# Wider matmuls for q, k and v: two narrow ones become one of 512 columns

## The chip, the cores and the metric

One core of a Trainium2 chip runs the whole program. The metric is device time in microseconds, from runs of the compiled kernel. TensorE (PE in the profile) multiplies 128x128 weights, loaded by a load instruction of their own (PEld), with a moving operand of up to 512 columns; it accumulates in PSUM, of which the kernel has eight buffers of 128x512 fp32. VectorE (DVE), ScalarE (ACT) and GpSimd (POOL) do the element-wise work, and the SP queue issues nearly all transfers from HBM.

## What is computed

Two decoder layers on 512 tokens of width 1024. Each has a token mixer and a squared-ReLU MLP, modulated by shift, scale and gate vectors that come from a conditioning vector (the adaLN products, "ada"). The parts that matter here, cut from the reference:

```python
# layer 0: the even mixer
proj = u @ w_in          # xr 512, yr 512, q 256, k 256, v 512, g 512, zl 16 columns
h = rg_lru(causal_dwconv(xr, ...), ...)
o = gla_chunked(q, k, v, log_alpha)          # 4 heads, chunks of 64 tokens
mix = concat([h * gelu(yr), rms_norm(o) * silu(g)]);  y = mix @ w_out
# layer 1: forgetting attention, 16 heads of 64
proj = u @ w_in          # q, k, v, g of 1024 columns each, 16 forget logits
q = rms_norm(q per head) * 64 ** -0.5;  k = rms_norm(k per head)
s = q @ k.T + f_cum[t] - f_cum[s], causal;  o = softmax(s) @ v
y = (o * sigmoid(g)) @ w_out
```

## The kernel before

**Products in three parts.** For fp32 precision each operand is split into a rounded high half and a low half, and a product is three matmuls: high by high, high by low, low by high (`mm3`). u is kept split and transposed (`uh`, `ul`; 8 blocks of 128 rows of the contraction). Projections whose result stands with tokens on partitions (`proj_tok`) take 128 tokens of u as weights and stream the columns of the weight matrix: 8 blocks x 3 = 24 matmuls for a token tile.

**Weights.** `plan_weights` lists all pieces of the weight matrices in the order of use, 1 MB each in the stages of this change. `w_dma` loads a piece into one of two staging buffers (`ws`); `w_pre` splits the next piece: ScalarE rounds it into `wh` (cast), VectorE subtracts for `wl`, in two tiles each, with four buffers for each of `wh` and `wl`, so two pieces exist at a time; `w_take` hands the next piece to its user and calls `w_pre` itself when the piece isn't split yet. A "tok" piece is 256 columns over the whole contraction of 1024 rows.

**Even mixer.** A string (`order`, L1051) writes out the order of the steps by hand: `q0` is a q product, `p` is `w_pre`, `t` a step of the ada products, `e` transposes of k, `R` the LRU gates, `s` scores, `g` the gate products, `S` the states, and so on. `v0` to `v7` are the products of v: four token tiles for the first 256 columns, then four for the second. Each is copied to its half of the tile `VV`.

**Attention.** The heads are worked through in groups j of four (256 columns of q, k and v). `stream` yields the projection units in order: q's four token tiles, k's, v's, for j = 1 to 3, then the gates. Group 0 is done before the heads begin. Strings (`orders`, L1532) mix one unit (`u`) at a time with the attention steps of a head: scores (`a`), decay (`d`), normalisation (`n`), transposes of the probabilities (`t`), values (`v`) and the stacking of the next q and k (`0` to `3`). `qk_units` puts two token tiles of q (or k) side by side into one PSUM buffer of 512 columns, and copies, squares and sums them; after all four tiles an rsqrt on VectorE and two multiplications on GpSimd normalise them.

Within these orders the tile framework still schedules: an engine's instruction order is fixed when the kernel is built, by priority of program order among what its own timing model holds ready. Helpers record all operations, so the profile gives one line (L50) for all; names of tiles tell them apart: `pqk` is q and k of the attention layer, `pfv` its v, `pfg` its gates, `pv` the even mixer's v, `pg` its gates, `pw` the output projections.

Of the kernel before, what the change touches and what calls it, by code (L numbers as in the profile page):

```python
# [8 lines left out]
F32 = mybir.dt.float32  # L9
F32R = mybir.dt.float32r  # L10
BF16 = mybir.dt.bfloat16
I32 = mybir.dt.int32
AF = mybir.ActivationFunctionType
ALU = mybir.AluOpType
AX = mybir.AxisListType
# [3 lines left out]
P = 128  # L19
D = 1024  # L20
S = 512
NT = S // P
# [4 lines left out]
RMS_EPS = 1e-6  # L27
# [7 lines left out]
WS_BUFS = 2  # L35
# [38 lines left out]
class Trunk:  # L74
# [19 lines left out]
    def s2(self, name, dtype=F32):  # L94
        return self.sp.tile([P, S], dtype, tag="s2", name=name)
# [220 lines left out]
    def plan_weights(self):  # L316
        i = self.i
        L = []
        win = i["ev_w_in"][0]
        L += [("ch", win, 1024, 256), ("ch", win, 1280, 256), ("tok", win, 1536), ("tok", win, 1792),  # L320
              ("ch", win, 2048, 256), ("ch", win, 2304, 256), ("ch", win, 640, 128), ("ch", win, 768, 256)]

        def out(w, n):
            for h in range(2):
                for b in range(2):
                    L.append(("half", w, h, b, n))

        def mlp(l):
            w1, w2 = i["mlp_w1"][l], i["mlp_w2"][l]
            up = lambda b: [("ch", w1, b * 512, 256), ("ch", w1, b * 512 + 256, 256)]  # L330
            dn = lambda b: [("rows", w2, b * 512, 2 * l + 1), ("rows", w2, b * 512 + 256, 2 * l + 1)]
            L.extend(up(0))
            for b in range(1, 8):
                L.extend(up(b) + dn(b - 1))
            L.extend(dn(7))

        self.wsmall = set()

        def alternate(n0):
            for q in range(n0, len(L)):  # L340
                if (q - n0) // 2 % 2:
                    self.wsmall.add(q)

        n0 = len(L)
        out(i["ev_w_out"][0], 0)
        mlp(0)
        alternate(n0)
        win = i["od_w_in"][0]
        tok = lambda m, j: ("tok", win, m * D + j * 256)
        L += [tok(0, 0), tok(1, 0), tok(2, 0)]  # L350
        for j in range(1, 4):
            L += [tok(0, j), tok(1, j), tok(2, j)]
        L += [("ch", win, 3 * D + j * 256, 256) for j in range(4)]
        n0 = len(L)
        out(i["od_w_out"][0], 2)
        mlp(1)
        alternate(n0)
        self.wlist, self.n_dma, self.n_split, self.n_take = L, 0, 0, 0
        self.wstage, self.wready = {}, {}

    def w_dma(self):
        d = self.wlist[self.n_dma]
        kind, w = d[0], d[1]
        if kind == "ch":
            shape, src = (KC, d[3]), w[:, d[2]:d[2] + d[3]]
        elif kind == "tok":
            shape, src = (KC, 256), w[:, d[2]:d[2] + 256]
        elif kind == "half":
            shape, src = (4, 512), w[d[3] * 512:d[3] * 512 + 512, d[2] * 512:d[2] * 512 + 512]
        else:  # L370
            shape, src = (2, D), w[d[2]:d[2] + 256, :]
        st = self.wp.tile([P, *shape], F32, tag="ws", bufs=WS_BUFS, name="ws")
        self.nc.sync.dma_start(st, src.rearrange("(k p) f -> p k f", p=P))
        self.wstage[self.n_dma] = st
        self.n_dma += 1
# [23 lines left out]
    def w_pre(self, eng=None):  # L399

        nc = self.nc
        if self.n_split >= len(self.wlist):
            return
        while self.n_dma < min(self.n_split + WS_BUFS, len(self.wlist)):
            self.w_dma()
        d = self.wlist[self.n_split]
        st = self.wstage.pop(self.n_split)
        kind = d[0]
        small = self.n_split in self.wsmall
        if kind == "ch":  # L410
            r = [self.split(st[:, :, m * P:m * P + P], P, small, eng) for m in range(d[3] // P)]
        elif kind == "tok":
            r = [x for h in range(2) for x in self.split(st[:, 4 * h:4 * h + 4, :], 256, small, eng)]
        elif kind == "half":
            r = []
            for a in range(2):
                r += self.split(st[:, 2 * a:2 * a + 2, :], 512, small, eng)
        else:
            r = []
            for k in range(2):  # L420
                for h in range(2):
                    s = st[:, k, h * 512:h * 512 + 512]

                    if d[2] >= DFF - 512:
                        nc.gpsimd.tensor_tensor(s, s, self.gates[d[3]][h], op=ALU.mult)
                r.append(self.split(st[:, k:k + 1], 512, small, eng))
        self.wready[self.n_split] = r
        self.n_split += 1
# [327 lines left out]
    def even(self):  # L756
        nc, tc, i, s2 = self.nc, self.tc, self.i, self.s2
# [14 lines left out]
        for m, nm in enumerate(("ev_rg_wa", "ev_rg_wx")):  # L772
            src = i[nm][0].rearrange("(q two) a b -> two a q b", two=2)
# [100 lines left out]
        W = {}  # L874
# [20 lines left out]
            nc.vector.tensor_tensor(ke[m], pk[m], E3[m], op=ALU.mult)  # L895

        V = [VV[:, t] for t in range(NT)]
        KE, kts = {}, {}

        def ke_t(t):  # L900

# [25 lines left out]
                AT[t, par] = at  # L927

        def v_proj(q):
            w2, t = q // 4, q % 4  # L930
            if t == 0:
                W["v"] = self.w_take()
            pt = self.ps("pv")
            self.proj_tok(pt[:, 0:256], W["v"], t)
            nc.scalar.copy(V[t][:, w2 * 256:w2 * 256 + 256], pt[:, 0:256])

        sg = {}

# [90 lines left out]
        ssq = [self.tiny.tile([P, 8], F32, tag="ss8", name="ss") for _ in range(2)]  # L1029
# [9 lines left out]
        def gla_put(h):  # L1039
            pt = self.ps("pot")  # L1040
            for t in range(NT):
# [6 lines left out]
        steps = dict(q=q_proj, D=decays, c=conv, M=lambda: nc.vector.tensor_copy(cm, cf), p=self.w_pre, t=self.tick,  # L1048
                     Q=q_decay, k=k_proj, K=k_decay, G=lambda: gelu(0, acc_ps[4]), v=v_proj, R=rg_gates, e=ke_t, s=scores,
                     g=silu, S=states, B=rg_sqrt, o=outs, n=norms, C=rg_scan, r=rg_put, y=yr, h=gla_put)  # L1050
        order = ("q0 c0 D M q1 p c1 t Q k0 p c2 K0 t k1 c3 K1 t G v0 p t e0 v1 R0 t e2 e1 v2 t v3 t e3 v4 "  # L1051
                 "p t s0 v5 t s1 R1 v6 t s2 v7 g0 t s3 t R2 p g1 R3 S0 t S2 g2 B p o0 o1 n0 t g3 C p t r0 "
                 "o2 o3 n2 y1 t y2 p t h0 p h2 h3 y3 t h1")
        for x in order.split():
            steps[x[0]](*[int(y) for y in x[1:]])
# [187 lines left out]
    def fox(self, rest):  # L1243
        nc, tc, i, s2 = self.nc, self.tc, self.i, self.s2
        win = i["od_w_in"][0]
# [18 lines left out]

            return unit

        def qk_units(j, m):

            w = self.w_take()
            pts = {}  # L1270
            QK[j, m] = [s2("qt") for _ in range(2)]
            ssq = self.tiny.tile([P, 16], F32, tag="ssq", name="ssq")

            def unit(t):
                b = t // 2
                if t % 2 == 0:
                    pts[b] = self.ps("pqk")
                pt, qt = pts[b], QK[j, m][b]
                self.proj_tok(pt[:, (t % 2) * 256:(t % 2) * 256 + 256], w, t)
                if t == 0:  # L1280
                    self.w_pre()
                if t % 2 == 0:
                    return
                sq = s2("sq")
                nc.scalar.copy(qt, pt)
                nc.scalar.activation(sq, pt, AF.Square)
                nc.vector.tensor_reduce(ssq[:, 8 * b:8 * b + 8], heads(sq), op=ALU.add, axis=AX.X)
                if b == 0:
                    return
                nc.vector.tensor_scalar(ssq, ssq, 1.0 / 64.0, RMS_EPS, op0=ALU.mult, op1=ALU.add)  # L1290
                r = self.rsqrt(ssq, 16)
                for q in range(2):
                    x = heads(QK[j, m][q])
                    rb = r[:, 8 * q:8 * q + 8].rearrange("p (a o) -> p a o", o=1).broadcast_to([P, 8, 64])
                    nc.gpsimd.tensor_tensor(x, x, rb, op=ALU.mult)

            return unit

        def stack(j, pr, m):

            pt = self.ps("pqt")
            for t in range(NT):
                c0 = (t % 2) * 256 + pr * P
                nc.tensor.transpose(pt[:, t * P:t * P + P], QK[j, m][t // 2][:, c0:c0 + P], self.ident)
            h0 = 4 * j + 2 * pr
            for hd in range(2):
                a, b = hd * 64, 64 - hd * 64
# [152 lines left out]


        wfs = forget_weights()
        u0 = qk_units(0, 0)
        u1 = qk_units(0, 1)
        for t in range(NT):
            u0(t)
            u1(t)
            if t == 0:
                rest(2)
            if t == 1:  # L1470
                rest(3)
        cols = forget()
        OG += [self.u8(f"og{k}", F32) for k in range(2)]
# [7 lines left out]

        def stream():
            for j in range(1, 4):
                for make in (lambda: qk_units(j, 0), lambda: qk_units(j, 1), lambda: v_units(j)):
                    u = make()
                    for t in range(NT):
                        yield lambda: u(t)
            for j in range(4):
                u = g_units(j)
                for m in range(2):  # L1490
                    for half in range(2):
                        yield lambda: u(m, half)
# [36 lines left out]
            "2": lambda h: stack(h // 4 + 1, 1, 0) if h < 12 else None,  # L1529
            "3": lambda h: stack(h // 4, 1, 1),  # L1530
        }
        orders = ("aduntu3uv", "datunuuv", "adnu0ut1uv", "audntu2uv")  # L1532
        for h in range(16):
            j, e = h // 4, h % 4
            for c in orders[e]:
# [61 lines left out]
```

## Time and profile before

| | us |
|---|---|
| median of 3 runs | 1263.17 (1262.27 to 1264.21) |
| profiled execution, its time | 1266.51 |
| its span, first to last instruction | 1264.8 |
| TensorE busy | 1224.6 |
| VectorE busy | 908.8 |
| ScalarE busy | 590.2 |
| GpSimd busy | 512.9 |

The profile is of one execution. Busy times count what an engine executes; matmuls overlap each other, so the distance between the starts of two tells what one costs in a row of them. A wait is put down to what ended it. The granted clock is that of TensorE, 1.00 being 2.4 GHz.

### The profile page before, as it was taken

To read this page: it belongs to the slowest core of one execution; us is meant where nothing else is said; L and a number is where in the kernel's file an instruction comes from. 1 tells how busy PE (TensorE), PEld (TensorE's weight loads), DVE (VectorE), ACT (ScalarE), POOL (GpSimd) and SP (SyncE) were. 2 spreads that over 40 slices of the span, in tenths; PEclk is the share of its full clock that TensorE was granted. 3 is DMA by queue.
4 is the path that set the end of the run, shared out by engine and by line. 5 is a ranking of instruction groups with operands and counts; after the bars stand their busy time and mean duration, and the time that the engine had idled before them with its cause. 6 is when DMAs were issued, how large, how long until landed. Compare 5 with 4: busy or idle time off the path is not lost. (4 is left out here: it accounts for less than half of the span.)

```text
span 1264.8 us, 17847 instructions
## 1 busy us (share of the span) xinstructions
PE 1224.6 (97%) x6543; PEld 1044.2 (83%) x6543; DVE 908.8 (72%) x1423; ACT 590.2 (47%) x1044; POOL 512.9 (41%) x524
## 2 busy tenths in 40 slices
PE   6999899999999999999999999999899999999997
PEld 5787678888888888888999999887888788888886
DVE  7689898768877866879578878778768744543656
ACT  3476653452453544432567767753453342322321
POOL 3665523346330321474266558558437000000166
PEclk9999999999999999999999999999999999999999
DMA  9657416163666466524232332343262624232311
GB/s 316 186 199 267 173 61 198 56 230 119 240 224 233 145 195 227 182 67 124 81 101 85 92 93 52 113 153 106 79 233 72 211 67 133 81 117 70 133 34 67
DMA packets 126409, 177.52 MB, mean 140 GB/s; under 512 B 9270, under 2 KB 82644, under 8 KB 126322
## 3 DMA queue, kind: packets, MB, share of 16 engines
q1 hardware_dynamic: 126210, 176.33, 42.4%
q8 instruction: 52, 0.85, 0.3%
q14 instruction: 35, 0.29, 0.1%
q10 hardware_dynamic: 112, 0.05, 0.0%
HBM read 172.10 MB, written 4.26 MB: 139 GB/s over the span
## 5 line engine op out<-in xcount | busy, mean ns | idle before, releaser
L50 DVE TENSOR_TENSOR wl<-ws,wh 128x512 fp32r<-128x512 f32 (+1 forms) x255 | 269.3, 1081 | 67.7 <-ACT wh L50 63.4
L50 ACT CAST wh<-ws 128x1024 fp32r<-128x1024 f32 (+2 forms) x271 | 207.5, 808 | 200.5 <-PE p L50 81.4
L50 PE MATMUL p<-uh,wh 128*128 128x512 f32 (+1 forms) x576 | 206.2, 366 | 0.0
L50 PE MATMUL p<-uh,wl 128*128 128x512 f32 (+1 forms) x576 | 205.9, 365 | 0.0
L50 PE MATMUL p<-wh,hh 128*128 128x512 f32 (+1 forms) x516 | 201.0, 390 | 0.0
L50 PE MATMUL p<-wh,hl 128*128 128x512 f32 (+1 forms) x516 | 200.0, 388 | 0.0
L50 PE MATMUL p<-wl,hh 128*128 128x512 f32 (+1 forms) x516 | 199.9, 387 | 0.0
L50 PE MATMUL p<-ul,wh 128*128 128x512 f32 (+1 forms) x576 | 192.9, 366 | 0.0
L50 POOL TENSOR_TENSOR acc<-acc,ast 128x512 f32<-128x512 f32 x70 | 102.9, 1470 | 203.3 <-ACT ast L50 108.4
L50 DVE TENSOR_TENSOR h<-r 128x512 f32<-128x512 f32 x64 | 53.6, 840 | 123.6 <-ACT r L50 123.6
L50 PEld LDWEIGHTS p<-uh,wl 128*128 128x128 f32 x576 | 108.6, 189 | 17.5
L50 PEld LDWEIGHTS p<-uh,wh 128*128 128x128 f32 x576 | 108.6, 189 | 17.6
L50 PEld LDWEIGHTS p<-ul,wh 128*128 128x128 f32 x576 | 100.9, 189 | 17.4
L50 PEld LDWEIGHTS p<-wh,hh 128*128 128x128 f32 x516 | 96.9, 188 | 20.3 <-issue 0.2
L50 PEld LDWEIGHTS p<-wl,hh 128*128 128x128 f32 x516 | 96.9, 188 | 20.2 <-issue 0.5
L50 PEld LDWEIGHTS p<-wh,hl 128*128 128x128 f32 x516 | 96.9, 188 | 19.8
L50 ACT ACTIVATE r<-p,colA 128x512 f32<-128x512 f32 x64 | 43.8, 684 | 148.7 <-PE p L50 148.7
L50 POOL TENSOR_TENSOR ws<-ws,gate 128x512 f32<-128x512 f32 x16 | 25.0, 1597 | 210.6 <-DMA ws<-in_mlp_w_dram 210.6
L50 DVE TENSOR_TENSOR Y<-Y,p 128x512 f32<-128x512 f32 x96 | 64.8, 681 | 41.0 <-PE p L50 40.3
L50 ACT ACTIVATE ast<-ast,cs 128x512 f32<-128x512 f32 x70 | 49.9, 721 | 91.3 <-DMA ast<-in_ada_w_dram 91.3
L50 DVE SCALAR_TENSOR_TENSOR acc<-ast,cs,acc 128x512 f32<-128x512 f32 x70 | 82.5, 1179 | 13.2 <-DMA ast<-in_ada_w_dram 12.7
L50 POOL TENSOR_TENSOR ul<-u,uh 128x512 fp32r<-128x512 f32 x32 | 45.0, 1418 | 74.0 <-ACT uh L50 65.4
(320 smaller groups left out, 2681.2 us busy)
## 6 DMA issues: line engine op xcount, KB each, us to landing
ws<-in_mlp_w_dram SPq DMA_DIRECT2D x64, 1024.0 KB
ast<-in_ada_w_dram SPq DMA_DIRECT2D x160, 256.0 KB
ws<-in_od_w_in_dram SPq DMA_DIRECT2D x16, 1024.0 KB
ast<-in_ada_w_dram SPq DMA_DIRECT2D x16, 512.0 KB
ws<-in_ev_w_in_dram SPq DMA_DIRECT2D x7, 1024.0 KB
ws<-in_ev_w_out_dram SPq DMA_DIRECT2D x4, 1024.0 KB
nf<-fd SPq DMA_DIRECT2D x16, 256.0 KB
ws<-in_od_w_out_dram SPq DMA_DIRECT2D x4, 1024.0 KB
```

What stands on the lines that cost most here:

```text
L50: x = f(*a, **k)
```

## The change

q and k of a group of four heads are computed by the same matmul: 256 columns of q and 256 of k stream as one operand of 512 columns, written to one PSUM buffer. The even mixer's v is computed in 512 columns at once. So that the split weights still fit, a piece no longer holds all 1024 rows of 256 columns but one half of the contraction (512 rows) of 512 columns: "wide" for the even mixer's v (contiguous), "two" for q and k (two transfers into one staging buffer; the tile holds q's two blocks and then k's, so that the streamed operand consists of two runs of 256 columns with a gap of 256 columns between them). A unit becomes a half unit (t, half) of 12 matmuls; its result is complete after the second half. In the attention layer the half units go in the order (0,0) (1,0) (0,1) (1,1) (2,0) (2,1) (3,0) (3,1), so two PSUM buffers are open at the beginning. Normalisation goes by pairs of token tiles, for q and k together. Two pieces are taken at a group's first unit, and the next piece is split after (3,0). In the even mixer both pieces of v are taken at `v0`; the `p` behind `v0` is dropped, the one behind `v4` moves behind `v6`, and one more stands behind `g0`.

```diff
-        L += [..., ("tok", win, 1536), ("tok", win, 1792),
+        L += [..., ("wide", win, 0, 1536), ("wide", win, 1, 1536),
...
-        L += [tok(0, 0), tok(1, 0), tok(2, 0)]
-        for j in range(1, 4):
-            L += [tok(0, j), tok(1, j), tok(2, j)]
+        for j in range(4):
+            L += [("two", win, a, j * 256) for a in range(2)] + [("tok", win, 2 * D + j * 256)]
...
+        elif kind == "wide":
+            shape, src = (4, 512), w[d[2] * 512:d[2] * 512 + 512, d[3]:d[3] + 512]
+        elif kind == "two":
+            st = self.wp.tile([P, 2, 4, 256], F32, tag="ws", bufs=WS_BUFS, name="ws")
+            for m in range(2):
+                self.nc.sync.dma_start(st[:, m], w[d[2] * 512:d[2] * 512 + 512, m * D + d[3]:m * D + d[3] + 256]
+                                       .rearrange("(k p) f -> p k f", p=P))
...
+        elif kind == "two":
+            r = []
+            for a in (0, 2):
+                hi, lo = [self.wp.tile([P, 2, 2, 256], F32R, tag=x, name=x) for x in ("wh", "wl")]
+                nc.scalar.copy(hi, st[:, :, a:a + 2])
+                nc.vector.tensor_tensor(lo, st[:, :, a:a + 2], hi.bitcast(F32), op=ALU.subtract)
+                r += [(hi[:, :, k], lo[:, :, k]) for k in range(2)]
...
         def v_proj(q):
+            t, half = q // 2, q % 2
+            if q == 0:
+                W["v"] = self.w_take() + self.w_take()
+            if half == 0:
+                vts[t] = self.ps("pv")
+            self.mm3(vts[t], [self.uk(k, t * P, t * P + P) + W["v"][k] for k in range(4 * half, 4 * half + 4)],
+                     half == 0, half == 1)
+            if half == 1:
+                nc.scalar.copy(V[t], vts.pop(t))
...
-        order = ("... G v0 p t e0 v1 R0 t e2 e1 v2 t v3 t e3 v4 "
-                 "p t s0 v5 t s1 R1 v6 t s2 v7 g0 t s3 t R2 p ...")
+        order = ("... G v0 t e0 v1 R0 t e2 e1 v2 t v3 t e3 v4 "
+                 "t s0 v5 t s1 R1 v6 p t s2 v7 g0 p t s3 t R2 p ...")
...
+        def qk_units(j):
+            w = self.w_take() + self.w_take()
+            pts, ssq = {}, {}
+            QK[j] = [s2("qt") for _ in range(NT)]
+            def unit(t, half):
+                b = t // 2
+                if half == 0:
+                    pts[t] = self.ps("pqk")
+                out = pts[t].rearrange("p (m f) -> p m f", m=2)
+                self.mm3(out, [self.uk(k, t * P, t * P + P) + w[k] for k in range(4 * half, 4 * half + 4)],
+                         half == 0, half == 1)
+                if half == 0:
+                    if t == NT - 1:
+                        self.w_pre()
+                    return
+                ...
+                nc.scalar.copy(x, pt)
+                nc.scalar.activation(sq, pt, AF.Square)
+                nc.vector.tensor_reduce(ssq[b][:, 8 * (t % 2):8 * (t % 2) + 8], heads(sq), op=ALU.add, axis=AX.X)
+                if t % 2 == 0:
+                    return
+                ... (mean square, rsqrt of 16 columns, two multiplications on GpSimd)
...
-        orders = ("aduntu3uv", "datunuuv", "adnu0ut1uv", "audntu2uv")
+        orders = ("aduntu3uv", "datunuuv", "adnuut0u1v", "audntu2uv")
```

## Rows read from the trace of the kernel before

**Rows 1.** The page's busy times, share of the span and instructions, by engine.

```profile
PE 1224.6 (97%) x6543; PEld 1044.2 (83%) x6543; DVE 908.8 (72%) x1423; ACT 590.2 (47%) x1044; POOL 512.9 (41%) x524
```

**Rows 2.** Stretches: length, then busy time of each engine, granted clock, DMA share, GB/s.

```profile
84.70:185.20 100.50, 91.50 (x596) 73.02 (x595) 90.47 (x135) 59.78 (x108) 46.27 (x32) 0.98 0.51 178
...
594.00:634.50 40.50, 40.50 (x326) 38.72 (x325) 22.36 (x60) 20.68 (x35) 11.69 (x11) 1.00 0.26 83
634.50:790.00 155.50, 155.13 (x1232) 151.60 (x1231) 126.09 (x312) 110.51 (x236) 97.66 (x178) 1.00 0.29 84
790.00:848.00 58.00, 56.73 (x301) 48.31 (x300) 39.89 (x83) 38.71 (x82) 29.83 (x47) 1.00 0.42 147
```

**Rows 3.** Waits of TensorE: us in total, times, longest.

```profile
PE po L50 <- DVE SS L50: 4.1, 1, 4.1
...
PE pot L50 <- DVE ot L50: 2.4, 2, 2.1
...
PE pfg L50 <- DVE mx L50: 1.3, 1, 1.3
PE pke L50 <- DVE ke L50: 1.2, 1, 1.2
```

**Rows 4.** Groups of instructions by shape: busy us, mean ns; idle before.

```profile
L50 PE MATMUL pqk<-wh,uh 128*128 128x256 f32 x256 | 74.1, 290 | 0.0
...
L50 PE MATMUL pfg<-uh,wh 128*128 128x512 f32 x64 | 25.8, 403 | 1.3 <-DVE mx L50 1.3
```

**Rows 5.** Timeline of TensorE, first q and k units: start us, duration us.

```profile
594.00 0.28 PE L50 MATMUL pqk<-wh,uh 128*128 128x256 f32 x1
594.11 0.28 PE L50 MATMUL pqk<-wl,uh 128*128 128x256 f32 x1
...
599.63 0.28 PE L50 MATMUL pqk<-wh,ul 128*128 128x256 f32 x1
```

**Rows 6.** Timeline of TensorE, second and 24th matmul of a gate unit.

```profile
820.32 0.40 PE L50 MATMUL pfg<-ul,wh 128*128 128x512 f32 x1
...
825.31 0.39 PE L50 MATMUL pfg<-uh,wl 128*128 128x512 f32 x1
```

**Rows 7.** Groups on ScalarE, copies out of PSUM: busy us, mean ns.

```profile
L50 ACT COPY qt<-pqk 128x512 f32<-128x512 f32 x16 | 9.5, 593 | 2.6 <-PE pqk L50 2.5
...
L50 ACT COPY VV<-pv 128x256 f32<-128x256 f32 x8 | 2.9, 363 | 3.1 <-PE pv L50 3.1
```

**Rows 8.** Timelines of three engines around the even mixer's first v unit.

```profile
84.71 0.28 PE L50 MATMUL pv<-wh,uh 128*128 128x256 f32 x1
...
87.52 1.03 ACT L50 CAST wh<-ws 128x1024 fp32r<-128x1024 f32 x1
...
92.68 2.28 DVE L50 TENSOR_TENSOR wl<-ws,wh 128x1024 fp32r<-128x1024 f32 x1
```

**Rows 9.** Timelines of ScalarE and VectorE, a later piece of the even mixer.

```profile
118.70 1.06 ACT L50 CAST wh<-ws 128x1024 fp32r<-128x1024 f32 x1
...
123.44 1.21 DVE L50 TENSOR_TENSOR wl<-ws,wh 128x1024 fp32r<-128x1024 f32 x1
```

**Rows 10.** Timeline of TensorE, attention work between units of the second group.

```profile
672.91 0.40 PE L50 MATMUL pov<-Ph,vs 128*128 128x512 f32 x1
...
675.46 0.28 PE L50 MATMUL pfv<-wh,uh 128*128 128x256 f32 x1
...
681.64 1.25 PE L50 MATMUL ppt<-ident,Sm 128*128 128x128 f32 x10
```

**Rows 11.** Timelines of ScalarE and VectorE, one piece of the attention layer.

```profile
664.95 1.05 ACT L50 CAST wh<-ws 128x1024 fp32r<-128x1024 f32 x1
...
670.38 1.21 DVE L50 TENSOR_TENSOR wl<-ws,wh 128x1024 fp32r<-128x1024 f32 x1
```

**Rows 12.** Issues of the attention layer's weight pieces on SP's queue: minimum, median, maximum ns.

```profile
L50 SPq DMA_DIRECT2D ws<-in_od_w_in_dram x16: 367/384/400, 552.1 to 787.5; - x16
```

**Rows 13.** Timeline of TensorE, first matmul of the second output projection.

```profile
848.20 0.39 PE L50 MATMUL pw<-wh,mh 128*128 128x512 f32 x1
```

More of the change, by code (lines that the diff above doesn't have):

```diff
@@ L319, in plan_weights @@
         win = i["ev_w_in"][0]
-        L += [("ch", win, 1024, 256), ("ch", win, 1280, 256), ("tok", win, 1536), ("tok", win, 1792),
+        L += [("ch", win, 1024, 256), ("ch", win, 1280, 256), ("wide", win, 0, 1536), ("wide", win, 1, 1536),
               ("ch", win, 2048, 256), ("ch", win, 2304, 256), ("ch", win, 640, 128), ("ch", win, 768, 256)]
@@ L348, in plan_weights @@
         win = i["od_w_in"][0]
-        tok = lambda m, j: ("tok", win, m * D + j * 256)
-        L += [tok(0, 0), tok(1, 0), tok(2, 0)]
-        for j in range(1, 4):
-            L += [tok(0, j), tok(1, j), tok(2, j)]
+        for j in range(4):
+            L += [("two", win, a, j * 256) for a in range(2)] + [("tok", win, 2 * D + j * 256)]
         L += [("ch", win, 3 * D + j * 256, 256) for j in range(4)]
@@ L367, in w_dma @@
             shape, src = (KC, 256), w[:, d[2]:d[2] + 256]
+        elif kind == "wide":
[5 more added lines that the diff above has]
+                                       .rearrange("(k p) f -> p k f", p=P))
+            self.wstage[self.n_dma] = st
+            self.n_dma += 1
+            return
         elif kind == "half":
@@ L413, in w_pre @@
             r = [x for h in range(2) for x in self.split(st[:, 4 * h:4 * h + 4, :], 256, small, eng)]
-        elif kind == "half":
+        elif kind == "two":
[5 more added lines that the diff above has]
+                r += [(hi[:, :, k], lo[:, :, k]) for k in range(2)]
+        elif kind in ("half", "wide"):
             r = []
@@ L897, in even @@
         V = [VV[:, t] for t in range(NT)]
-        KE, kts = {}, {}
+        KE, kts, vts = {}, {}, {}
         def ke_t(t):
@@ L929, in v_proj @@
         def v_proj(q):
[L930 to L935, printed above, removed]
+            t, half = q // 2, q % 2
[7 more added lines that the diff above has]
+                nc.scalar.copy(V[t], vts.pop(t))
         sg = {}
@@ L1050, in even @@
                      g=silu, S=states, B=rg_sqrt, o=outs, n=norms, C=rg_scan, r=rg_put, y=yr, h=gla_put)
-        order = ("q0 c0 D M q1 p c1 t Q k0 p c2 K0 t k1 c3 K1 t G v0 p t e0 v1 R0 t e2 e1 v2 t v3 t e3 v4 "
-                 "p t s0 v5 t s1 R1 v6 t s2 v7 g0 t s3 t R2 p g1 R3 S0 t S2 g2 B p o0 o1 n0 t g3 C p t r0 "
+        order = ("q0 c0 D M q1 p c1 t Q k0 p c2 K0 t k1 c3 K1 t G v0 t e0 v1 R0 t e2 e1 v2 t v3 t e3 v4 "
+                 "t s0 v5 t s1 R1 v6 p t s2 v7 g0 p t s3 t R2 p g1 R3 S0 t S2 g2 B p o0 o1 n0 t g3 C p t r0 "
                  "o2 o3 n2 y1 t y2 p t h0 p h2 h3 y3 t h1")
@@ L1265, in v_units @@
             return unit
[L1267 to L1274, printed above, removed]
-                b = t // 2
-                if t % 2 == 0:
[L1277 to L1281, printed above, removed]
+        def qk_units(j):
[3 more added lines that the diff above has]
+            def unit(t, half):
+                b = t // 2
+                if half == 0:
[7 more added lines that the diff above has]
+                    return
+                if t % 2 == 0:
+                    ssq[b] = self.tiny.tile([P, 16], F32, tag="ssq", name="ssq")
+                pt, sq, x = pts.pop(t), s2("sq"), QK[j][t]
+                nc.scalar.copy(x, pt)
+                nc.scalar.activation(sq, pt, AF.Square)
+                nc.vector.tensor_reduce(ssq[b][:, 8 * (t % 2):8 * (t % 2) + 8], heads(sq), op=ALU.add, axis=AX.X)
@@ L1282, in unit @@
                 if t % 2 == 0:
                     return
[L1284 to L1291, printed above, removed]
+                nc.vector.tensor_scalar(ssq[b], ssq[b], 1.0 / 64.0, RMS_EPS, op0=ALU.mult, op1=ALU.add)
@@ L1292, in unit @@
+                r = self.rsqrt(ssq[b], 16)
                 for q in range(2):
-                    x = heads(QK[j, m][q])
+                    x = heads(QK[j][2 * b + q])
                     rb = r[:, 8 * q:8 * q + 8].rearrange("p (a o) -> p a o", o=1).broadcast_to([P, 8, 64])
@@ L1302, in stack @@
             for t in range(NT):
-                c0 = (t % 2) * 256 + pr * P
-                nc.tensor.transpose(pt[:, t * P:t * P + P], QK[j, m][t // 2][:, c0:c0 + P], self.ident)
+                c0 = m * 256 + pr * P
+                nc.tensor.transpose(pt[:, t * P:t * P + P], QK[j][t][:, c0:c0 + P], self.ident)
             h0 = 4 * j + 2 * pr
@@ L1462, in fox @@
         wfs = forget_weights()
[L1463 to L1468, printed above, removed]
+        HALVES = [(0, 0), (1, 0), (0, 1), (1, 1), (2, 0), (2, 1), (3, 0), (3, 1)]
+        u0 = qk_units(0)
+        for q, th in enumerate(HALVES):
+            u0(*th)
+            if q == 0:
                 rest(2)
-            if t == 1:
+            if q == 2:
                 rest(3)
@@ L1483, in stream @@
             for j in range(1, 4):
[L1484 to L1487, printed above, removed]
+                u = qk_units(j)
+                for th in HALVES:
+                    yield lambda: u(*th)
+                u = v_units(j)
+                for t in range(NT):
+                    yield lambda: u(t)
             for j in range(4):
```

## The prediction

> **What bounds the kernel now.** I read the page's busy shares first: TensorE is busy 1224.6 of 1264.8 us, VectorE 908.8 [rows 1]. An average over stages says little about one edit, so next comes the table of stretches around the two places that the change touches. In the attention layer TensorE has work in 40.50 of 40.50 us, then 155.13 of 155.50, then 56.73 of 58.00; in the even mixer only 91.50 of 100.50, while VectorE is at 90.47 there [rows 2]. The granted clock is 1.00 in the attention stretches, the 2.4 GHz level. The waits of TensorE say where its idle time ends: in the even mixer 4.1 us for VectorE's state updates and 2.4 us for its normalised outputs, in the attention layer the longest is 1.3 us [rows 3]. So a nanosecond taken from a matmul of the attention layer is a nanosecond of the kernel; one taken in the even mixer ahead of the wait for the states is probably waited out there.
>
> Durations can't price the matmuls. A 256-column one shows some 290 ns, a 512-column one some 403 [rows 4], but they overlap, so distances between starts count. From the second to the 48th start of the first two q and k units are 46 steps in 599.63 − 594.11 = 5.52 us: 120.0 ns each [rows 5]. From the second to the 24th start of a 512-column gate unit are 22 steps in 825.31 − 820.32 = 4.99 us: 226.8 ns each [rows 6]. Two narrow matmuls cost 240.0 ns, one wide one 226.8, so a merged pair saves 13.2 ns.
>
> **The change part by part.** *q and k.* Before, 4 head groups × 2 matrices × 4 token tiles = 32 units of 24 narrow matmuls, 2.880 us each. After, 4 × 4 × 2 = 32 half units of 12 wide ones, 2.722 us. Saved: 32 × 0.158 = 5.07 us, in stretches where TensorE does not wait. There are as many units as before, so I count nothing for switches between units and attention work. What follows a unit keeps its count and size: 4 × 4 copies of 512 columns, as the 16 before [rows 7], and likewise the squares and reductions; the tiles only hold q and k of one token tile instead of two token tiles of q.
>
> *The wide operand comes in two runs of 256 columns with a gap.* No matmul of this trace streams such a pattern. Bounds: nothing, as the contiguous wide matmul, or the price of two separate matmuls, 240.0 ns, which takes the 5.07 us away. A loss beyond that would need an extra cost for the break itself, for which no row speaks. I take nothing, since the break is one in 512 columns.
>
> The Trainium skill, TensorE: Matmul & The Clock Gate, section "Back-to-back issue gap", puts the isolated gap at N/2.4 + 2.5 ns; by that a pair would save 2.5 ns and 384 pairs 0.96 us, giving 1262.2 us instead of 1258.1. The rows disagree on both widths (120.0 against its 109.2, 226.8 against 215.8 ns), and I go by the rows.
>
> *The even mixer's v.* Eight units of 24 become eight half units of 12: 8 × 0.158 = 1.27 us, but ahead of the 4.1 us wait for the states. VectorE is busy 90% of that stretch and keeps all its work, so I count 0; bounds 0 and 1.27. ScalarE's eight copies of 363 ns become four of some 593, 0.5 us less, off the path [rows 7].
>
> *Weights by halves of the contraction, the even mixer.* Now the second piece must be there for the second half unit, where it used to be needed only at the fifth unit. Its rounding takes two casts and two subtractions. The second cast starts at 87.52 and its subtraction, queued on VectorE behind convolutions, k's decays and adaLN sums, runs from 92.68 for 2.28 us, to 94.96 [rows 8]. v starts at 84.71; the first half unit ends at 87.43, and after 6 more matmuls (1.36 us) the second reaches rows from the second tile, at 88.8. If TensorE stood there until 94.96 it would lose 6.2 us. What is queued behind v1 on TensorE are the gate products of the LRU, for which ScalarE and then VectorE wait. But the program order lets the first half unit of the next tokens (2.72 us), the gate products and the transposes of k be put in between, work that TensorE did in that interval anyway, and 1.2 us of it was already idle before k's transpose [rows 3]. Bounds 0 and 6.2; I take 0, as later waits of 4.1 and 2.4 us can absorb a short loss.
>
> *The gate weights of the even mixer.* Their rounding moves from behind v4 to behind v6, whose buffers it needs; then v7, 2.72 us, and one score step cover it, where three units did before. Cast plus subtraction alone are 1.06 + 1.21 us, but from 118.70, where one cast starts, it took until 123.44 + 1.21 = 124.65, 5.95 us [rows 9]. Bounds 0 and 5.95 − 2.72 = 3.2 us; I take 0, for the same reason. The extra rounding at the first v step is only an earlier call: one piece more is prepared before the output projection.
>
> *Weights in the attention layer.* v's rounding moves from the first k unit to the last first-half unit, and what remains before v's first matmul is one half unit, 2.72 us, and the attention work between: values and scores of a head 675.46 − 672.91 = 2.55, ten transposes 1.25 us [rows 10]; together 6.5, and 1.4 more until the second tile is reached. From the first cast to the end of the second subtraction the trace shows 664.95 to 671.59, 6.6 us [rows 11]. It just fits: I take 0, bound 1 us for each of three groups. The group's second q/k piece is taken at its first unit and needed two units later, with as much attention work between; 0. Each paired piece has two transfers in place of one: 8 × 0.38 us more of issuing on the SP queue [rows 12] over some 220 us, ahead of loads that are due a unit later; 0. For the first group, half of the rsqrt chains now comes two units earlier, off the end; no gain counted since TensorE had forget-gate work there.
>
> **The sum.** Against the profiled execution, 1266.51 us (span 1264.8): 1266.51 − 5.07 = 1261.44. That execution lies 3.34 us above the median of the runs, so for the median: 1263.17 − 5.07 = 1258.1 us.
>
> **The rivals.**
> (a) *The gap in the operand costs as much as a second matmul.* Then the change does not do what it says: starts of the q/k matmuls stand 240 ns apart, no time is saved in the attention layer, 1263.2 us. For it: nothing shows the pattern. Against it: each run is as long as a whole narrow matmul.
> (b) *Late rounding in the even mixer, the slower side.* Place: the second tile of v's second piece, and the gate weights behind v6; one mechanism, VectorE's queue between cast and subtraction. For it: VectorE is at 90% there and the lags above. Against it: TensorE has other products to put between, and waits later anyway. Price up to 6.2 + 3.2 = 9.4 us; it decides for slower above 5.07 + 2.5 = 7.6. At the full price 1263.17 − 5.07 + 9.4 = 1267.5; with v1's stall alone 1264.3.
> (c) *The cover in the attention layer is short.* v's first unit waits 1 us in each of three groups: 1261.1. For it: 6.5 against 6.6 us. Against it: TensorE's order already mixes attention work between units, and both engines have free time (VectorE 126 of 155 us [rows 2]).
>
> **How the numbers follow.** Forecast 0.55 (own range 1256.8, where v's 1.27 us counts too, to 1260.6, where a stall of under 2.5 us does); (a) 0.07; (b) beyond 7.6 us 0.13, and smaller, between 2.5 and 7.6, 0.13; (c) 0.12. A difference of 0.2%, 2.5 us, is about what a measurement can tell from none. Faster: the forecast and 0.8 of (c), 0.65. Same: (a), the smaller (b) and the rest of (c), 0.22. Slower: 0.13. The range goes down to all gains whole, 5.07 + 1.27, and the attention layer's wait of 1.3 us gone, 1255.5; up to v1's whole stall, 1264.3. What lies above it is most of the slower side.
>
> **What would show it.** Starts of the merged q/k matmuls 227 ns apart, 384 of them where 768 stood; the stretch from the first q/k matmul to the output projection, 594.00 to 848.20 before [rows 5, 13], some 5.1 us shorter; no TensorE wait for the rounding of weights at v; the wait for the states about 1.3 us longer, or the even mixer ending where it did. Wrong if the starts stand 240 ns apart, if TensorE waits for a subtraction of weights in the first v units or at g, or if the attention layer shows new waits at v's first unit.

## The result: 1.6% slower

The changed kernel takes 1285.6 us (median of 4 runs, 1281.7 to 1286.6) against 1263.7 (1262.3 to 1265.5) for the kernel before: a ratio of 1.016, 95% interval 1.0143 to 1.0177. The forecast was 1258.1 us (range 1255.5 to 1264.3). The profiled execution has a span of 1283.6 us, 18.8 more than before.

Busy times do not show it: TensorE 1235.0 us (10.4 more than in [rows 1], of which some is the same work at a lower clock), VectorE 904.0, ScalarE 590.8. The first matmuls of three tiles (`pv`, `pw`, `pqk`) cut the span into stages that can be compared: v of the even mixer, first output projection, first q/k matmul, second output projection. What lies ahead of v is 0.8 us longer.

| us | v to output projection | output projection and MLP 0 | attention layer | from the second output projection to the end |
|---|---|---|---|---|
| before | 100.53 | 408.76 | 254.20 | 416.60 |
| changed | 102.82 | 419.20 | 260.91 | 415.12 |

The largest loss, 10.4 us, lies in a stage in which no line of code was changed. The attention layer, where 5.1 us were to be gained, is 6.7 us longer.

The product itself does what was forecast. TensorE's timeline of the changed kernel, second to 13th merged matmul (start, duration in us):

```profile
607.79 0.39 PE L50 MATMUL pqk<-wl,uh 128*128 128x512 f32 x1
...
610.28 0.39 PE L50 MATMUL pqk<-wh,uh 128*128 128x512 f32 x1
```

11 steps in 2.49 us are 226 ns each, as for the contiguous operand of [rows 6]. There are 384 such matmuls. The losses stand in the waits of TensorE (us in total, times, longest):

```profile
PE pada L50 <- ACT acch L50: 5.8, 1, 5.8
PE po L50 <- DVE SS L50: 3.5, 2, 2.5
PE pada L50 <- DVE accl L50: 2.9, 1, 2.9
PE pv L50 <- DVE wl L50: 2.8, 1, 2.8
PE pov L50 <- DVE Pl L50: 2.2, 2, 1.3
PE pfv L50 <- DVE og L50: 2.1, 2, 1.0
PE pov L50 <- ACT Ph L50: 1.6, 1, 1.6
```

Of these `po` alone is in [rows 3]; the wait for Pl was 0.4 us before. `pada` is the column sum of an adaLN product in MLP 0: the sums it needs were late. `pv <- wl` is v's second piece. `pov` are the values of the attention, waiting for the probabilities' split halves Ph and Pl; `og` is VectorE's reading of the values out of PSUM. The windows around them (length, busy time of TensorE, its weight loads, VectorE, ScalarE, GpSimd, granted clock, DMA share, GB/s), first the two stalls of MLP 0, then one in the attention layer:

```profile
348.40:352.40 4.00, 1.44 (x5) 1.15 (x6) 2.94 (x5) 0.00 (x0) 0.00 (x0) 0.89 0.26 85
352.40:356.40 4.00, 4.00 (x14) 3.15 (x13) 1.29 (x2) 2.62 (x4) 1.50 (x2) 0.68 0.31 117
484.40:488.40 4.00, 1.62 (x8) 0.99 (x6) 1.55 (x3) 0.00 (x0) 0.00 (x0) 0.96 0.22 75
488.40:492.40 4.00, 0.61 (x2) 0.52 (x3) 2.28 (x3) 1.28 (x2) 0.00 (x0) 0.50 0.21 66
492.40:496.40 4.00, 4.00 (x14) 3.18 (x13) 3.69 (x5) 2.18 (x3) 0.00 (x0) 0.69 0.24 67
...
764.00:768.00 4.00, 2.44 (x15) 1.76 (x14) 1.21 (x4) 3.84 (x12) 1.25 (x4) 1.00 0.00 0
768.00:772.00 4.00, 4.00 (x15) 3.65 (x16) 3.80 (x11) 2.97 (x6) 4.00 (x10) 0.58 0.02 4
```

Each of these three stalls is paid twice: TensorE stands, and in the 4 us after it, busy again, it is granted 0.58 to 0.69 of its clock on average, partly the 1.2 GHz level. Before, TensorE had no wait and a granted clock of 1.00 from 230 to 594 us:

```profile
230.00:594.00 364.00, 364.00 (x1712) 304.79 (x1711) 277.98 (x344) 161.55 (x262) 142.87 (x98) 1.00 0.52 171
```

### The profile page after: what moved, and what is told of

Its sections match the earlier page's. It is cut to its first block, busy times and chain, and to the rows that moved or that the text cites. A ratio compares the mean times of both kernels' runs of the same rounds, so it can differ in the third digit from the quotient of the medians.

```text
span 1283.6 us, 16888 instructions
## 1 busy us (share of the span) xinstructions
PE 1235.0 (96%) x6063; PEld 1027.2 (80%) x6063; DVE 904.0 (70%) x1421; ACT 590.8 (46%) x1040; POOL 513.6 (40%) x526
## 4 chain that ended last, share of the span: by engine, by line
PE 69%; DVE 15%; DMA 6%; issue 4%; ACT 3%; SPq 2%; POOL 1%; DVEq 0%; ACTq 0%; POOLq 0%
PE p L50 46%; PE pqk L50 6%; DMA ast<-in_ada_w_dram 4%; PE pfv L50 4%; PE pfg L50 3%; DVE wl L50 3%; SPq L50 2%; DVE acc L50 2%; DVE X L50 2%; PE psc L50 1%; PE pov L50 1%; PE pw L50 1%; PE ppt L50 1%; PE pv L50 1%; DVE mod L50 1%
## 5 line engine op out<-in xcount | busy, mean ns | idle before, releaser
L50 ACT CAST wh<-ws 128x512 fp32r<-128x512 f32 (+2 forms) x271 | 208.4, 808 | 162.1 <-PE p L50 83.0
L50 DVE TENSOR_TENSOR h<-r 128x512 f32<-128x512 f32 x64 | 50.2, 785 | 101.3 <-ACT r L50 101.3
```

The source lines that it names most:

```text
L50: x = f(*a, **k)
```

## The experiments

Three questions: what disturbs MLP 0, what makes the attention layer longer although its matmuls are cheaper, and what the wide v costs. The stage lengths of all kernels, cut as above:

| us | v to output proj. | MLP 0 | attention | median | ratio to before, 95% interval |
|---|---|---|---|---|---|
| e1 one piece less | 102.58 | 408.17 | 259.24 | 1272.4 | 1.0061 (1.0040 to 1.0081) |
| e2 q and k alone | 100.53 | 408.75 | 259.68 | 1271.4 | 1.0053 (1.0037 to 1.0068) |
| e3 before, piece more | 100.41 | 418.60 | 254.08 | 1276.5 | 1.0090 (1.0055 to 1.0124) |
| e4 units apart | 103.73 | 407.33 | 262.80 | 1273.7 | 1.0077 (1.0050 to 1.0104) |
| e5 v's lo on GpSimd | 99.51 | 407.71 | 276.79 | 1282.1 | 1.0162 (1.0137 to 1.0187) |
| e6 two narrow products | 101.50 | 408.06 | 253.62 | 1264.6 | 1.0018 (1.0005 to 1.0032) |
| e7 tile by tile | 100.26 | 408.62 | 256.58 | 1267.6 | 1.0040 (1.0026 to 1.0055) |
| e8 rounding spread | 99.10 | 408.51 | 260.69 | 1271.4 | 1.0065 (1.0048 to 1.0083) |
| e9 wide, narrow order | 100.54 | 407.94 | 253.44 | 1264.4 | 1.0014 (1.0001 to 1.0027) |
| e10 narrow, wide order | 100.69 | 406.54 | 262.41 | 1275.3 | 1.0094 (1.0079 to 1.0109) |
| e11 wide v crossed | 100.62 | 408.02 | 252.95 | 1261.7 | 0.9989 (0.9977 to 1.0002) |
| e12 all engines' order | 100.25 | 408.38 | 249.80 | 1259.8 | 0.9968 (0.9956 to 0.9980) |
| e13 fewer tiles | 100.25 | 410.20 | 254.28 | 1263.3 | 1.0000 (0.9986 to 1.0014) |
| e15 ada by GpSimd | 115.36 | 413.60 | 254.72 | 1294.4 | 1.0260 (1.0223 to 1.0298) |

Each stage length is that of one profiled execution. Stages whose code is the same differ between kernels: the even mixer with the old v takes 99.1 to 101.5 us, MLP 0 with the old count of pieces 406.5 to 408.8, the attention layer of before 254.1 to 254.7.

### MLP 0: e1, e3, e13, e15

The order string has nine `p` before and after. But v0 now takes two pieces, and a take prepares what is not yet prepared; so one piece more is split by the time of the output projection, and weights stay one piece further ahead throughout MLP 0.

e1, the changed kernel less one preparation:

```diff
-                 "o2 o3 n2 y1 t y2 p t h0 p h2 h3 y3 t h1")
+                 "o2 o3 n2 y1 t y2 p t h0 h2 h3 y3 t h1")
```

> The changed kernel with one preparation (the p behind h0) taken out of the even mixer's order, so that at the output projection the weights are again prepared as far ahead as before the change. Theory A, the extra piece prepared ahead is what disturbs MLP 0: from the first output projection to the first q/k matmul back from 419.2 to 408.8 us (+-1), no wait of TensorE for the adaLN sums there, granted clock 1.00; whole kernel some 1275 us. Theory B, the stalls in MLP 0 come from the shifted times alone, however many pieces are ahead: that stretch stays at 416 us or more, whole kernel 1282 or more. The even mixer's own loss of 3.1 us stays under both. If the attention layer also drops below 258 us, the extra piece cost there as well.

Measured: MLP 0 408.17 us, no wait for adaLN sums, and a median of 1272.4 us where the changed kernel has 1285.6. Its stage in one window:

```profile
187.70:595.70 408.00, 405.91 (x1900) 338.83 (x1899) 315.88 (x403) 179.47 (x291) 154.00 (x103) 1.00 0.52 172
```

e3, the reverse, the kernel before with one preparation more:

```diff
-                 "p t s0 v5 t s1 R1 v6 t s2 v7 g0 t s3 t R2 p g1 ...
+                 "p t s0 v5 t s1 R1 v6 t s2 v7 g0 p t s3 t R2 p g1 ...
```

> The kernel before the change with one preparation more (a p behind g0, where the changed kernel has one), nothing else. Theory A: MLP 0 shows the waits for the adaLN sums and the half clock, first output projection to first q/k matmul about 419 instead of 408.8 us, whole kernel 1272 to 1276. Theory B: no stalls, 1263 +-1.5.

Measured: 418.60 us, and the waits are back in a kernel that has none of the new products:

```profile
PE pada L50 <- ACT acch L50: 4.6, 1, 4.6
PE pada L50 <- DVE accl L50: 2.8, 2, 2.7
```

Theory A holds both ways: the extra piece is worth some 10 us in this stage (11.0 and 9.8). How does a piece that is ready *earlier* make sums late? The SP queue of e3 and then of the kernel before, from 318 us (start, us, transfer), and what e3's queue waited for between 318.4 and 326.2:

```profile
318.58 0.33 SPq L50 DMA_DIRECT2D gb<-in_ada_b_dram  x1
325.98 0.38 SPq L50 DMA_DIRECT2D ws<-in_mlp_w_dram  x1
326.45 0.89 SPq L50 DMA_DIRECT2D ast<-in_ada_w_dram  x2
```

```profile
319.78 1.78 SPq L50 DMA_DIRECT2D ast<-in_ada_w_dram  x2
321.82 0.33 SPq L50 DMA_DIRECT2D gb<-in_ada_b_dram  x1
322.93 3.73 SPq L50 DMA_DIRECT2D ast<-in_ada_w_dram  x4
```

```profile
SPq L50 <- DVE wl L50: 7.0, 1, 7.0
```

A load of MLP weights (`ws`) stands at the head of the queue for 7.0 us until VectorE has freed its staging buffer, and the adaLN loads (`ast`) come behind it. This wait alone doesn't tell the two kernels apart, though. Before, such loads waited for `wl` as well, in MLP 0 even longer in total, and e3's next column sum begins earlier, not later (its first term on ScalarE at 327.47 us, before at 329.40). What is new stands behind that point, in the waits of the adaLN loads themselves. Waits of the SP queue from 186 to 600 us, e3 and then before:

```profile
SPq L50 <- DVE wl L50: 179.3, 35, 16.8
SPq L50 <- POOL acc L50: 56.2, 10, 8.0
SPq L50 <- DVE accl L50: 28.9, 9, 5.0
```

```profile
SPq L50 <- DVE wl L50: 203.1, 35, 27.3
...
SPq L50 <- POOL acc L50: 3.4, 4, 1.2
```

In all, the adaLN loads wait 103 us in e3 and 57 before. VectorE's last terms of the sum for which TensorE then waits 4.6 us wait for such loads:

```profile
483.00 0.75 DVE L50 SCALAR_TENSOR_TENSOR acc<-ast,cs,acc 128x512 f32<-128x512 f32 x1 [2.79 <-DMA ast<-in_ada_w_dram]
...
486.44 0.75 DVE L50 SCALAR_TENSOR_TENSOR acc<-ast,cs,acc 128x512 f32<-128x512 f32 x1 [1.50 <-DMA ast<-in_ada_w_dram]
```

`acc` on GpSimd and `accl` are the last to read 128x512 tiles of the kind that the adaLN loads fill, so these loads wait until such a tile is free. That is a second way: the buffers. A prepared piece of the small kind holds such tiles too, eight of them by the kernel's `split` (four of `wh`, four of `wl`; the expectation below counts four). e13 takes four tiles from the kernel before:

```diff
-S2_BUFS = 42
+S2_BUFS = 38
```

> The kernel before the change with 38 instead of 42 buffers of 128x512 (S2_BUFS), nothing else; an additional prepared piece of the small kind holds four of these. Theory I, the extra piece disturbs MLP 0 because its tiles are missing to the adaLN loads and sums: the same waits of TensorE for acch and accl and the half clock there, first output projection to first q/k matmul 415 us or more instead of 408.8. Theory J, the extra piece disturbs by its staging transfer and its place in the SP queue, not by the tiles that it holds: 408 to 411 us. Only that stretch is compared, since the attention layer uses these buffers too.

Measured: 410.20 us, no wait for acch or accl. Four missing tiles do not do it; but that is half of what the extra piece holds, so theory I is not refuted. e15 is e3 with the adaLN loads on another queue:

```diff
-                nc.sync.dma_start(st, w[r * P:r * P + P, cb * 512:cb * 512 + 512])
+                nc.gpsimd.dma_start(st, w[r * P:r * P + P, cb * 512:cb * 512 + 512])
```

> The kernel before the change with one preparation more, as e3_before_plus_piece, and the adaLN weights (ast) loaded through GpSimd's queue instead of SP's. In e3 a load of MLP weights stands in SP's queue from 319 to 326 us waiting 7.0 us for a staging buffer (wl), and the adaLN loads come after it. Theory J, that queue is how the extra piece reaches the adaLN sums: without it no wait of TensorE for acch and accl of more than 1 us, first output projection to first q/k matmul 408 to 411 us instead of 418.6. If the sums are late for another reason (their buffers, or ScalarE and GpSimd themselves), the waits stay: 415 us or more.

Measured: in MLP 0 the waits for acch and accl shrink from 7.4 to 1.2 us, but the stage takes 413.6, with a new wait of 3.8 us for VectorE's Y; and in the even mixer a column sum waits 15.6 us. The waits in question shrink, as theory J has it, but the stage's length lies between the two expectations; that GpSimd now holds loads and sums in one order is a likely reason, not a shown one. Late adaLN loads are the way to the late sums. Whether they are late for want of buffers, as the waits of e3 say, or by the order of the queue, as e15 suggests, no run separates: none takes eight tiles away.

### The attention layer: e2, e4 to e10, e12

e2 keeps of the change only q and k (even mixer as before):

> Only the q and k part of the change, in the attention layer; the even mixer with its v by 256 columns and its order of steps as before the change. Theory A (extra piece) and theory B (shifted times) alike: first q/k matmul again at about 594, as before. For the attention layer: if the merged products save what their starts say, 249 us from the first q/k matmul to the output projection and 1258 in all; if the new order of half units leaves TensorE without filling work, as in the changed kernel, 258 to 261 us and some 1268 to 1270.

Measured: attention 259.68 us, 5.5 us longer than before. So the loss belongs to q and k. e4 is e1 with `"adnu0ut1uv"` again in place of `"adnuut0u1v"`:

> As e1_one_piece_less, and in the attention layer the order of a head's steps again with a projection unit between the stacking of q and k and before the values, adnu0ut1uv in place of adnuut0u1v. Theory C, the values wait because no projection matmul is left between the transposes and them: the waits for Ph and half of the clock drops go, attention layer 3 us shorter than in e1. Theory D, the rounding of weights on VectorE ahead of Pl and the half units themselves are the cause: within 1 us of e1.

Measured: 262.80, 3.6 us longer than e1, where theory C expected 3 us less and theory D no change; the wait for Ph is still 1.6 at one place, those for Pl rise from 2.3 to 3.6. Theory C in this form falls: the letters of that string are not the lever. The next four change e2.

e5:

```diff
                     if t == NT - 1:
-                        self.w_pre()
+                        self.w_pre(nc.gpsimd)
```

> As e2_qk_alone, but the subtraction that splits v's weights runs on GpSimd instead of VectorE (three times two tiles of 128x1024). Theory D, weight rounding bunched on VectorE ahead of the subtraction Pl delays the values: the waits of TensorE for Pl (2.3 us in e2) go and with them the half clock behind, attention layer some 255 to 256.5 us instead of 259.7. Theory C, the place of the projection matmuls among the attention steps is what counts: within 1 us of 259.7, the waits move to another place.

Measured: 276.79 us; waits for Pl 5.0 us, og 5.6, Ph 3.2, all longer. Against theory D, as far as it goes: the build laid the instructions in another order here too, so the run does not price the subtraction alone.

e8 moves `self.w_pre()` in v's units from `t == 0` to `t == 1`:

> As e2_qk_alone, but the next group's first q/k piece is prepared at v's second unit instead of its first, one unit further from the preparation of v. Theory D (bunched rounding ahead of Pl): the waits for Pl fall from 2.3 to under 1 us, attention 256 to 258 us. Theory C: within 1 us of 259.7.

Measured: 260.69, waits for Pl 2.2. This run tells nothing of theory D: on TensorE, VectorE, ScalarE and GpSimd its trace shows the same instructions in the same order as e2's. It is e2 once more, and shows that one order can take 259.7 or 260.7 us.

e7 sets `HALVES = [(t, h) for t in range(NT) for h in range(2)]`:

> As e2_qk_alone, with the half units in the plain order (t, 0), (t, 1): a token tile is finished before the next begins. Theory E, the crossed order (0,0) (1,0) (0,1) (1,1) keeps two PSUM buffers open and finishes two tiles in a row, so copies and squares come in bursts: attention 2 to 4 us shorter than 259.7. Rival: the second piece of weights is now needed one unit earlier and comes late, a wait for wl at the second half unit of each group, 1 to 3 us each: 262 us or more.

Measured: 256.58, 3.1 us better, as theory E said; but the waits for Pl are unchanged (2.3 us), so bursts are at most part of it.

e6 replaces the merged matmul by two, everything else staying:

```diff
-                self.mm3(out, [self.uk(k, t * P, t * P + P) + w[k] for k in ...], half == 0, half == 1)
+                for k in range(4 * half, 4 * half + 4):
+                    uh, ul = self.uk(k, t * P, t * P + P)
+                    for q, (x, y) in enumerate(((uh, w[k][0]), (uh, w[k][1]), (ul, w[k][0]))):
+                        for m in range(2):
+                            nc.tensor.matmul(pts[t][:, m * 256:m * 256 + 256], x, y[:, m], ...)
```

> As e2_qk_alone with everything of the new staging, order and follow-up work, but each merged 512-column matmul is again two of 256 columns into the two halves of the PSUM buffer. It prices the product by itself: if a merged pair saves 13.2 ns also inside this order, the attention layer is 5.1 us longer than in e2, some 264.8 us, and the kernel 1276. If the merged matmuls themselves do harm (fewer places where other work can be put between), it is as long as in e2 or shorter, and the waits for Ph and Pl are gone.

Measured: 253.62, *faster* than with the merged matmul by 6.1 us, and without the waits. The new staging and the half units cost nothing; with merging it is slower. What differs besides the matmuls is the order in which TensorE's instructions were laid when the kernel was built. Here is e2 at the values of the first head, then e6:

```profile
659.86 0.40 PE L50 MATMUL pqk<-wh,ul 128*128 128x512 f32 x1
660.10 0.40 PE L50 MATMUL pov<-Ph,vs 128*128 128x512 f32 x1
...
662.35 0.44 PE L50 MATMUL pov<-Pl,vs 128*128 128x384 f32 x1 [1.37 <-DVE Pl L50]
...
663.82 0.39 PE L50 MATMUL pov<-Pl,vs 128*128 128x256 f32 x1 [0.91 <-DVE Pl L50]
...
664.21 0.68 PE L50 MATMUL psc<-qk 128*128 128x256 f32 x3
```

```profile
659.77 0.33 PE L50 MATMUL pov<-Ph,vs 128*128 128x384 f32 x1
659.94 0.40 PE L50 MATMUL pqk<-wh,uh 128*128 128x256 f32 x2
...
660.59 0.28 PE L50 MATMUL pov<-Pl,vs 128*128 128x256 f32 x1
...
661.06 0.40 PE L50 MATMUL pqk<-wh,ul 128*128 128x256 f32 x2
```

In e6 projection matmuls stand between and behind the values; in e2 the group's last half unit is used up ahead of them, and TensorE has nothing else while VectorE makes Pl. e9 and e10 separate order from product: the orders of the two builds are exchanged, by dependencies without semaphores between successive instructions of TensorE in the attention layer.

```diff
+        for a, b in zip(seq, seq[1:]):     # seq: the other kernel's order of these instructions
+            self.tc.add_manual_dep(rec[b].ins, rec[a].ins.name, mybir.DependencyInfo(
+                mybir.DependencyClass.NoSync, mybir.DependencyReason.DATA), reason="given order")
```

> As e2_qk_alone (merged products, even mixer as before), but TensorE's instructions of the attention layer are held in the order that e6_two_narrow_products had, a merged matmul standing where the first of its two narrow ones stood. Theory G, the loss lies in the order that was fixed when the kernel was built, in which other work comes after the projection matmuls are used up: the waits for Pl, Ph and og go, granted clock 1.00 from 648 to 800, attention layer 253.6 - 5.1 = 248.5 us (247.5 to 250.5), kernel about 1259. Theory F, merged products make TensorE faster than VectorE and ScalarE can follow, in any order: waits of several us remain, attention 253 us or more.

> The counterpart: as e6_two_narrow_products (two narrow matmuls instead of each merged one), but TensorE's instructions of the attention layer held in the order that e2_qk_alone had; the other engines' orders are those of e2 too. Theory G: the waits stay although the products are narrow, attention 259 to 264 us, kernel 1271 or more. Theory F: as e6, attention 253 to 255 us, kernel 1264.

e12 does the same for VectorE, ScalarE and GpSimd as well (with the even mixer of e11, below):

> As e11_wide_v_crossed, but in the attention layer not only TensorE, also VectorE, ScalarE and GpSimd are held in the order of e6_two_narrow_products. In e9 and e11 the values, transposes and scores took 3.1 us longer than in e6 although TensorE kept its order (sums of the distances between starts), among it 1.0 us of waiting for a memset of kl on GpSimd, whose order was another. Theory H, those 3.1 us come from the other engines' changed orders: attention layer 250 to 251 us, kernel 1258.5 to 1260. Theory F, what the products save TensorE waits for the softmax chain in any order: attention 252.5 us or more, kernel as e11.

Distances between starts of TensorE's instructions in the attention layer, summed by tile (us):

| order, product | q/k | values | transposes of probabilities | scores | stage |
|---|---|---|---|---|---|
| e6: narrow order, narrow | 94.7 | 19.0 | 16.0 | 21.6 | 253.62 |
| e12: narrow order on all engines, merged | 90.9 | 18.9 | 15.9 | 21.6 | 249.80 |
| e9: narrow order on TensorE alone, merged | 91.3 | 20.1 | 17.5 | 22.1 | 253.44 |
| e2: its own order, merged | 90.7 | 22.2 | 19.5 | 22.6 | 259.68 |
| e10: e2's order, narrow | 94.4 | 22.0 | 18.9 | 22.7 | 262.41 |

Down the first column the product decides, across the next the order. Narrow products in e2's order (e10) wait just as merged ones do:

```profile
PE pov L65 <- DVE Pl L65: 1.9, 2, 1.0
PE pov L65 <- ACT Ph L65: 1.5, 1, 1.5
PE pfv L65 <- DVE og L65: 1.4, 2, 0.7
```

That is theory G. e9 took back only 6.2 of the expected 11 us, and its 253.44 lies where theory F had it, though the waits for Ph and og were gone; there GpSimd's order was still its own, and the first scores waited 1.0 us for its memset of `kl`. With the orders of all four engines given (e12) the layer takes 249.80 us, less than theory F allows, so F falls. The merged product brings 253.62 − 249.80 = 3.8 us, and the stage has two short waits left:

```profile
PE pfg L88 <- ACT tg L88: 0.5, 1, 0.5
PE ppt L88 <- DVE mx L88: 0.3, 1, 0.3
```

```profile
593.00:842.80 249.80, 249.06 (x1471) 217.88 (x1469) 188.60 (x453) 169.69 (x353) 136.62 (x236) 1.00 0.31 100
```

### The wide v: e11

The changed kernel at v's second piece, VectorE and TensorE:

```profile
93.46 2.28 DVE L50 TENSOR_TENSOR wl<-ws,wh 128x1024 fp32r<-128x1024 f32 x1
```

```profile
95.79 0.79 PE L50 MATMUL pv<-wl,uh 128*128 128x512 f32 x1 [2.79 <-DVE wl L50]
```

```profile
92.00:96.00 4.00, 0.87 (x5) 0.63 (x6) 4.00 (x4) 0.00 (x0) 2.57 (x2) 0.94 0.00 0
96.00:100.00 4.00, 3.92 (x9) 2.62 (x10) 4.00 (x7) 2.31 (x6) 0.00 (x0) 0.50 0.74 236
```

This is the place of rival (b), with the subtraction as late as in [rows 8]. e11 crosses the half units and has e1's count of preparations and e9's attention layer:

```diff
-        order = ("... G v0 t e0 v1 R0 t e2 e1 v2 t v3 ...
+        order = ("... G v0 t e0 v2 R0 t e2 e1 v1 t v3 ...
```

> As e9_wide_in_narrow_order in the attention layer, with the changed kernel's wide v in the even mixer, its preparations counted as in e1_one_piece_less, and its half units crossed: first halves of tokens 0 and 1, then their second halves (v0 v2 v1 v3 in the order). In e1 the even mixer took 102.6 us from v to the output projection against 100.5 before, with a wait of 2.2 us for the second piece's wl. If that wait is the price of needing the second piece at the second half unit, one half unit more ahead of it (2.7 us) takes it away: 100 to 100.6 us. If the wide v costs for another reason, 102 or more.

Measured: 100.62 us, no wait for the second piece. The three kernels with the uncrossed wide v take 102.6 to 103.7 us, the two with the crossed one (e11, e12) 100.3 and 100.6. So some 2 us were the price of needing it at the second half unit; that is no more than the old v's stage differs between kernels, and the wait that went is the firmer sign.

e12 is the version that beats both kernels: 0.9968 of before (0.9956 to 0.9980), 1259.8 us.

## Why the prediction was wrong

**The product: right in kind, a quarter too large.** The pitch of 226.8 ns came out (226), the operand in two runs costs nothing, rival (a) is out. The gain of 384 pairs was put at 5.07 us; where the four engines' orders are equal in the attention layer (e6, e12) it is 3.8, give or take the 1 us by which e8 differs from e2. By the isolated gap of the Trainium skill (TensorE: Matmul & The Clock Gate, section "Back-to-back issue gap") the gain would be 0.96 us, an estimate; these traces do not agree.

**The first step that failed: "The extra rounding at the first v step is only an earlier call: one piece more is prepared before the output projection."** It was seen and counted at nothing. It costs 10.4 us in MLP 0 (e1, e3), over half of the 18.8 us between the two profiled executions: adaLN loads come late, the sums come late, and the clock falls behind each of the two stalls. That the piece does this is shown; how it delays the loads is not settled. The waits of e3's queue speak for the 128x512 tiles that a small piece holds and the loads lack, e15 for the order of the queue. The prediction had looked at SP's queue in the attention layer alone, and at no buffers.

**The second: "There are as many units as before, so I count nothing for switches between units and attention work."** The number was right; what was missing is that the build laid another order on all engines for the merged matmuls. With the same units and follow-up work, the order of the merged build costs 262.41 − 253.62 = 8.8 us with narrow products, 259.68 − 249.80 = 9.9 with merged ones. That TensorE "does not wait" there, at 155.13 of 155.50 us busy [rows 2], was a property of that order, not of the layer. Why the build chose as it did for merged matmuls was not examined.

**Rival (b): right place, smaller price.** v's second piece was waited for: 2.8 us, then half a clock. In the end some 2 us of the 6.2 bound, since later waits in the stage shrank (`po` from 4.1 to 3.5, `pot` from 2.4 to none). It is the smallest of the three losses. Crossing takes it away. The chance of 0.13 for slower stood for this rival; the two larger losses were in none, so that part of the chances had the right side for the wrong reason.

**Rival (c)** did not occur: no wait for wl at v's first unit in the attention layer. That unit did wait anew in two of the groups, 2.1 us together, but for `og`.

## What to carry to other kernels

Count how many pieces are in flight after an edit of a staged pipeline: a call that prepares on demand changes the depth, and the buffers held, for every stage behind it, and the bill can come in code that nobody touched. Where instruction order is computed at build time, compare the order itself before pricing a cheaper instruction, and test the two apart by giving one build the order of the other. A busy engine without waits shows that its present order is good, not that it will stay so. And before a run is read, see in the trace whether the edit changed what the engines execute: e8's did not.

## What was not expected of the hardware

A matmul that streams two runs of 256 columns with a gap of 256 between them costs what a contiguous one of 512 does (226 ns). The granted clock often adds to a stall: after two waits of 1.4 and 0.9 us around 663 in e2 TensorE, fully busy again, was granted 0.63 in the next 4 us; after the wait of 1.56 us at 767 in the changed kernel 0.58, though after one of the same length at 753 in e2 it stayed at 1.00.
